# Two result tiles by turns for the expert blocks of a mixture-of-experts stage

## The chip, the core and the metric

The kernel runs on one core of one Trainium2 chip. The metric is the time of one execution on the device in microseconds (us); several runs of the same program are shown by their median. Five engines work side by side, each through its own list of instructions: PE (TensorE, matrix products into PSUM), ACT (ScalarE), DVE (VectorE), POOL (GpSimd, which here issues the gathers and scatters of single rows) and SP (SyncE, which here issues the plain transfers). An instruction that must wait holds up all that stand behind it in its engine's list.

## The reference

One decoder layer on 2048 tokens of width 1024: sliding-window attention beside a chunkwise mLSTM, an output projection, a cross attention to 256 memory slots, a mixture of experts, and a last RMSNorm. What the change touches is the mixture:

```python
hb = jax.nn.silu(xb @ w_g[e]) * (xb @ w_u[e])     # xb: the rows of the tokens of expert e
y = (hb @ w_d[e]) * gate                          # 1024 -> 512 -> 1024
out = zeros((t, d)).at[token].add(y)              # every token goes to two of 32 experts
out = rms_norm(x + out, norm_final)
```

All arithmetic is in float32. The kernel splits every float32 operand into a high and a low part and makes three products of them.

## The kernel before

The expert stage (`phase3`) runs over the 32 experts in a fixed order; x is the place in that order, 0 to 31. Each place x has these blocks of tokens:

- the full block: the first 128 tokens of the expert. `full_gate` and `full_up` make gate and up, `full_down` (with `down_turn`) makes the result in two PSUM tiles of 512 columns, ACT copies both into the tile `yA` in SBUF (line 1755), and POOL adds its rows into the table `y_d` in HBM with an indirect transfer (`add_rows`, line 1788);
- the half block: 64 more tokens, if the expert has more than 128. It stands in the If path of a branch (`half_within`, line 1693); its result goes into `hu`, the upper 64 partitions of the tile `both`. An expert with at most 128 tokens takes the Else path;
- the rare blocks: 64 tokens each, if the expert has more than 192 (`later_blocks`, a branch inside the If path, line 1719; a loop for more than 256 behind a further branch, line 1726). Their result goes into `yA[:64]`. These blocks need the first eight of the twelve weights again, whose split parts have been overwritten: they are read once more through two tiles by turns, `again` and `yA` (`reload`, line 1521), first four of this expert's, then four of the next expert's.

With this seed fifteen places up to 30 take the If path, sixteen the Else path, and one place (x = 2) runs a rare block.

Weights come from HBM in pieces of 512 KB (twelve an expert) into nine buffers `we_raw`; SP issues a piece when its buffer is free. ACT casts a piece to its high part (line 76), DVE makes the low part (line 77). On either path of the branch SP issues four pieces (`splitter(todo[:4])`), the fourth of them a piece of `w_e_up`. Behind the branch stand, in the order written for PE, ACT and DVE: the down products, four casts, the two copies of line 1755, the first products of the next expert (`full_gate`) with four casts and the silu, then its up products, which write the PSUM tiles that the copies read.

POOL's list holds, for each place: the gather of rows for the last norm where a group of experts is done (`sums`, line 1933, which reads `y_d` and so waits for the scatter before it; 15 places between 10 and 29), the gather of the next rows (line 1585), the small steps of the norm, its part of the branch, and the scatter of line 1788.

The waits are put in by the compiler. A transfer tells of its end by raising a counter once its data is in; there are eight such counters for SP's transfers and eight for POOL's, used by turns. What stands behind a branch waits for what either path may have done to its tile. So that a constant can be waited for, the path that did not issue a transfer raises that transfer's counter by hand, at its end (instructions of the lines 1460 and 1719) or ahead of a transfer of its own on the same counter.

Of the kernel before, what the change touches and what calls it, by code (L numbers as in the profile page):

```python
# [31 lines left out]
HB = 64  # L32
# [11 lines left out]
def together(*parts):  # L44

    parts = [iter(p) for p in parts]
    while parts:
        parts = [p for p in parts if next(p, p) is not p]


def by(n, part):

    for i, _ in enumerate(part):
        if i % n == n - 1:
            yield
# [11 lines left out]
class Net:  # L67
# [1675 lines left out]
    def down_turn(self, pd, hT, x, ws, step, norm, late):  # L1743
        for k in range(4):
            self.down(pd, hT, ws, (k,))
            step(2 if k == 1 else 1)
            self.steps(norm, k == 2, late[k])
        info = self.infos[x][0]
        y = self.sums_of.get("A", self.yA)
        for n in range(2):  # L1750
            yn = y[:, n * 512:n * 512 + 512]
            if self.sums_of:
                self.nc.vector.tensor_tensor(out=yn, in0=pd[n], in1=yn, op=ALU.add)
            else:
                self.nc.scalar.copy(out=yn, in_=pd[n])  # L1755
        if self.sums_of:
            out = [(info, self.yA), *self.due]
            self.due = []
            ssq, r = self.stats(P, len(out))
            self.square(y, ssq, 0)  # L1760
            self.gain(self.nc.vector, y, self.yA)
            root = self.root_steps(ssq, r)
            next(root)
            next(root)
            for at, y in out[1:]:
                self.gain(self.nc.vector, y)
            together(by(2, root), norm)
            for j, (at, y) in enumerate(out):
                rj = r[:y.shape[0], j:j + 1]
                if j:  # L1770
                    self.nc.scalar.activation(out=y, in_=y, func=AF.Copy, scale=rj)
                else:
                    self.nc.vector.tensor_scalar(out=y, in0=y, scalar1=rj, scalar2=None, op0=ALU.mult)
                self.give_apart(at, y)
        else:
            self.add_rows(info, y)
# [67 lines left out]
    def half_block(self, tg, info, ws):  # L1844

        h, u, hT = self.half_tiles()
        y = self.yA[:HB, :]
        if self.sums_of:
            self.sums(info, self.sums_of["L"])
        pg = self.pd()  # L1850
        self.gate(pg, tg, ws)
        self.half_silu(h, pg)
        self.half_up(h, u, tg, ws, info)
        pd = [self.pd() for _ in range(2)]
        for f in range(2):
            self.turn_h(h, hT, f)
            self.down(pd, hT, ws, (2 * f, 2 * f + 1))
        self.half_out(y, pd, info, "L")
# [183 lines left out]
```

## Time and profile before

| | |
|---|---|
| median of 3 runs | 2264.99 us (2260.93 to 2270.77) |
| the profiled execution | 2258.9 us, its span 2257.2 us |
| mean granted TensorE clock | 0.963 |
| expert stage | from about 1290 us to the end of the span |
| busy share of the span | PE 91%, DVE 69%, ACT 56%, POOL 21% |

The span goes from the first to the last instruction that the profile holds; the 1.7 us around it belong to the execution's time. Times in the rows count from the span's start.

### The profile page before, as it was taken

The numbers are of one execution on the slowest core, as the hardware profiler recorded it, in microseconds if no ns is written. First come the engines' busy times: TensorE is split into PE (matmuls) and PEld (weight loads), VectorE is DVE, ScalarE is ACT, GpSimd is POOL, SyncE is SP. The second block draws the span as 40 slices with busy tenths as digits, with TensorE's granted clock in tenths as the row PEclk, the third lists the DMA queues.
The fourth block names the chain that finished last, engine by engine and source line by source line (L and its number), as shares of the span: only waits on it lengthen the run. The fifth ranks groups of instructions, "written<-read, shape, count | busy, mean of one in ns | idle before, by whom it ended". The sixth has DMA issues, their size and how long they took to land. (4 is left out here: it accounts for less than half of the span.)

```text
span 2257.2 us, 36582 instructions
## 1 busy us (share of the span) xinstructions
PE 2055.1 (91%) x12173; PEld 1776.2 (79%) x12173; DVE 1555.3 (69%) x3586; ACT 1271.4 (56%) x2479; POOL 466.6 (21%) x536
## 2 busy tenths in 40 slices
PE   6999999999989999999997397799999999899894
PEld 5888888998867887889997285588877887778783
DVE  6277877278866666567777565486777778777764
ACT  6266886268874333355554154476666666666663
POOL 1000000000000000023332211021232426543335
PEclk9999999999999999999999699799999999999997
DMA  5533435443377897523545576496878979897853
GB/s 166 136 112 104 127 101 164 128 112 108 101 196 219 231 227 186 182 103 92 135 77 166 106 258 210 133 351 228 287 266 294 355 235 329 317 355 239 288 185 95
DMA packets 266261, 434.73 MB, mean 193 GB/s; under 512 B 53232, under 2 KB 175216, under 8 KB 265952
## 3 DMA queue, kind: packets, MB, share of 16 engines
q1 hardware_dynamic: 245216, 381.25, 54.8%
q0 software_dynamic: 20736, 49.85, 8.1%
q8 instruction: 134, 2.20, 0.4%
q14 instruction: 175, 1.43, 0.2%
HBM read 356.97 MB, written 92.71 MB: 199 GB/s over the span
## 5 line engine op out<-in xcount | busy, mean ns | idle before, releaser
L77 DVE TENSOR_TENSOR we_lo<-we_raw,we_hi 128x1024 fp32r<-128x1024 f32 x384 | 447.9, 1219 | 95.5 <-ACT we_hi L76 83.7
L76 ACT CAST we_hi<-we_raw 128x1024 fp32r<-128x1024 f32 x384 | 381.9, 1058 | 69.9 <-PE pd L1620 29.8
L125 PE MATMUL pu<-we_hi,xTA 128*128 128x256 f32 x512 | 149.7, 292 | 32.9 <-ACT yA L1755 32.9
L125 PE MATMUL mm<-hT,w_hi 128*128 128x512 f32 x416 | 166.4, 401 | 0.9 <-ACT hT L327 0.9
L126 PE MATMUL mm<-hT,w_hi 128*128 128x512 f32 x416 | 166.0, 399 | 0.0
L127 PE MATMUL mm<-hT,w_lo 128*128 128x512 f32 x416 | 165.9, 399 | 0.0
L127 PE MATMUL mm<-w_hi,hT 128*128 128x324 f32 (+1 forms) x512 | 152.6, 298 | 0.0
L125 PE MATMUL mm<-w_hi,hT 128*128 128x324 f32 (+1 forms) x512 | 152.5, 298 | 0.0
L126 PE MATMUL mm<-w_lo,hT 128*128 128x324 f32 (+1 forms) x512 | 152.1, 297 | 0.0
L126 PE MATMUL pu<-we_lo,xTA 128*128 128x256 f32 x512 | 148.6, 290 | 0.0
L127 PE MATMUL pu<-we_hi,xTA 128*128 128x256 f32 x512 | 148.6, 290 | 0.0
L589 POOL TENSOR_TENSOR sq<-sq 128x256 f32<-128x256 f32 x16 | 12.6, 787 | 588.4 <-ACT sq L586 588.4
L125 PEld LDWEIGHTS pu<-we_hi,xTA 128*128 128x128 f32 x512 | 101.6, 199 | 37.0 <-ACT yA L1755 35.9
L125 PE MATMUL pu<-we_hi,hT 128*128 128x512 f32 x256 | 106.0, 414 | 5.4 <-ACT both L1798 2.2
L126 PE MATMUL pu<-we_lo,hT 128*128 128x512 f32 x256 | 105.1, 410 | 5.2 <-PEq L1719 5.2
L127 PE MATMUL pu<-we_hi,hT 128*128 128x512 f32 x256 | 103.2, 403 | 0.0
L126 PEld LDWEIGHTS pu<-we_lo,xTA 128*128 128x128 f32 x512 | 101.5, 198 | 1.1
L125 PE MATMUL pg<-we_hi,xTA 128*128 128x512 f32 x256 | 101.8, 397 | 0.0
L126 PE MATMUL pg<-we_lo,xTA 128*128 128x512 f32 x256 | 101.4, 396 | 0.0
L127 PE MATMUL pg<-we_hi,xTA 128*128 128x512 f32 x256 | 101.3, 396 | 0.0
L127 PEld LDWEIGHTS pu<-we_hi,xTA 128*128 128x128 f32 x512 | 101.3, 198 | 0.0
L1788 POOL DMA_INDIRECT y_d<-yA,infoA x31 | 71.9, 2320 | 126.0 <-ACT yA L1755 64.6
(508 smaller groups left out, 6081.3 us busy)
## 6 DMA issues: line engine op xcount, KB each, us to landing
we_raw<-in_w_e_gate_dram SPq DMA_DIRECT2D x128, 512.0 KB
we_raw<-in_w_e_up_dram SPq DMA_DIRECT2D x128, 512.0 KB
we_raw<-in_w_e_down_dram SPq DMA_DIRECT2D x128, 512.0 KB
w_raw<-in_w_in_dram SPq DMA_DIRECT2D x56, 256.0 KB
q_in<-q_d SPq DMA_DIRECT2D x32, 256.0 KB
qk_d<-acc SPq DMA_DIRECT2D x32, 256.0 KB
at_d<-at SPq DMA_DIRECT2D x32, 256.0 KB
at_in<-at_d SPq DMA_DIRECT2D x32, 256.0 KB
```

Source lines behind the costliest of these rows:

```text
L76: first = nc.scalar.copy(out=hi, in_=src)
L77: (low or nc.vector).tensor_tensor(out=lo, in0=src, in1=hi.bitcast(F32), op=ALU.subtract)
L125: first = mm(ps, lhsT=wh, rhs=xh, start=start, stop=False)
L126: mm(ps, lhsT=wh, rhs=xl, start=False, stop=False)
L127: mm(ps, lhsT=wl, rhs=xh, start=False, stop=stop)
L589: nc.gpsimd.tensor_tensor(out=sq[:, 0:2], in0=sq[:, 0:2], in1=sq[:, 2:4], op=ALU.add)
L1788: self.nc.gpsimd.indirect_dma_start(out=self.y_d[:, :], out_offset=bass.IndirectOffsetOnAxis(ap=info[:, 0:1], axis=0), in_=y, in_offset=No ...
```

## The change

The full block's result goes into `yA` at even places and into `again` at odd ones. The rare blocks' result goes into `hu`, which holds the same block's gate and up before. Nothing else is edited; at the last place (31) the results go another way (`sums_of`), before as after.

```diff
     def down_turn(self, pd, hT, x, ws, step, norm, late):
...
         info = self.infos[x][0]
-        y = self.sums_of.get("A", self.yA)
+        y = self.sums_of.get("A", (self.yA, self.again)[x % 2])
...
     def half_block(self, tg, info, ws):
 
         h, u, hT = self.half_tiles()
-        y = self.yA[:HB, :]
+        y = self.hu
```

`reload` is not edited, and goes on using both tiles:

```python
        t = (self.again, self.yA)[i % 2]
        self.load_part(x, i, t)
        self.split(*w, t)
```

## Rows read from the trace of the kernel before

**Rows 1.** Stretches: from:to, length, busy us by engine, clock, DMA share, GB/s.

```profile
1455.00:1515.00 60.00, 60.00 (x347) 52.63 (x347) 51.84 (x57) 45.23 (x61) 13.57 (x10) 0.98 1.00 344
...
1875.00:1918.00 43.00, 42.16 (x233) 37.08 (x234) 36.22 (x44) 32.70 (x46) 24.58 (x21) 0.93 0.97 337
```

**Rows 2.** Line 1755: what ended ACT's idle time before it; who waited for it.

```profile
  DMA y_d<-yA,infoA: 15.4, 3
  DMA out_dram<-y_fin,list: 14.3, 2
  SPq L1719: 12.6, 12
...
  PE pu L125: 32.9, 7
```

**Rows 3.** Timeline of PE: start, us, line, operation [idle before, releaser].

```profile
1452.26 0.58 PE L125 MATMUL pu<-we_hi,xTA 128*128 128x256 f32 x1 [11.84 <-ACT yA L1755]
...
1659.30 0.45 PE L1782 MATMUL pt<-ident,hA 128*128 128x128 f32 x1 [3.16 <-DVE hA L1644]
...
1874.72 0.58 PE L125 MATMUL pu<-we_hi,xTA 128*128 128x256 f32 x1 [4.21 <-ACT yA L1755]
...
1969.16 0.58 PE L125 MATMUL pu<-we_hi,xTA 128*128 128x256 f32 x1 [5.29 <-ACT yA L1755]
...
2015.09 0.38 PE L125 MATMUL pu<-we_hi,xTA 128*128 128x256 f32 x1 [1.69 <-ACT yA L1755]
```

**Rows 4.** Timeline of POOL: the rare block's scatter, a full one, the gather behind.

```profile
1433.17 1.43 POOL L1788 DMA_INDIRECT y_d<-yA,infoB  x1 [25.43 <-DVEq L1726]
...
1760.80 1.84 POOL L1788 DMA_INDIRECT y_d<-yA,infoA  x1 [3.95 <-ACT yA L1755]
1771.34 1.02 POOL L1933 DMA_INDIRECT y_fin<-y_d,list  x1 [8.70 <-DMA y_d<-yA,infoA]
```

**Rows 5.** Instructions of line 1460 (Else path's end), 1776 to 1790 us: duration, starts.

```profile
L1460 POOLq INC_SWDGE_SEM  x1: 683/683/683, 1784.2 to 1784.2; - x1
```

**Rows 6.** Timeline of ACT: casts and copies of line 1755 at five places.

```profile
1511.32 0.58 ACT L1755 COPY yA<-pu 128x512 f32<-128x512 f32 x1
...
1761.62 1.05 ACT L76 CAST we_hi<-we_raw 128x1024 fp32r<-128x1024 f32 x1 [0.15 <-DMA we_raw<-in_w_e_gate_dram]
...
1784.99 0.59 ACT L1755 COPY yA<-pu 128x512 f32<-128x512 f32 x1 [4.56 <-DMA y_d<-yA,infoA]
...
1815.68 0.59 ACT L1755 COPY yA<-pu 128x512 f32<-128x512 f32 x1 [0.62 <-SPq L1719]
...
1988.40 0.59 ACT L1755 COPY yA<-pu 128x512 f32<-128x512 f32 x1
```

**Rows 7.** Timeline of SP: issues of reloads and of weight pieces.

```profile
1416.08 0.33 SPq L1516 DMA_DIRECT2D again<-in_w_e_up_dram  x1
...
1437.01 0.33 SPq L1516 DMA_DIRECT2D yA<-in_w_e_up_dram  x1
...
1443.10 0.33 SPq L1516 DMA_DIRECT2D yA<-in_w_e_up_dram  x1
...
1508.87 0.33 SPq L1516 DMA_DIRECT2D we_raw<-in_w_e_up_dram  x1
...
1753.78 0.33 SPq L1516 DMA_DIRECT2D we_raw<-in_w_e_gate_dram  x1
...
1811.22 0.33 SPq L1516 DMA_DIRECT2D we_raw<-in_w_e_up_dram  x1
...
1985.90 0.33 SPq L1516 DMA_DIRECT2D we_raw<-in_w_e_up_dram  x1
```

**Rows 8.** Stretches of 8 us behind two of the waits (columns as above).

```profile
1874.00:1882.00 8.00, 7.28 (x38) 7.28 (x39) 5.12 (x5) 6.68 (x11) 4.02 (x3) 0.57 0.79 249
...
1969.00:1977.00 8.00, 7.84 (x52) 7.84 (x52) 5.28 (x6) 6.22 (x11) 3.47 (x2) 0.75 0.81 253
```

**Rows 9.** The page's costliest group: busy us, mean ns of one, idle before.

```profile
L77 DVE TENSOR_TENSOR we_lo<-we_raw,we_hi 128x1024 fp32r<-128x1024 f32 x384 | 447.9, 1219 | 95.5 <-ACT we_hi L76 83.7
```

## The prediction

> **What bounds the kernel now.** I read the stretches of the expert stage first. Where several places in a row take the Else path, PE is busy nearly all the time (60.0 of 60 us) and the transfers run at 337 to 344 GB/s with 0.97 to 1.00 of the DMA engines' time [rows 1]. Two limits lie on top of each other there: what frees PE meets the transfers at once. That they do bind shows at 1761.62: the cast waited for its own piece, issued at 1753.78, so 7.8 us earlier [rows 6, 7].
>
> Then I read the copies of line 1755, since they alone write the tile that is doubled. PE waited for them seven times, 32.9 us together [rows 2], out of some 960 us of stage. One of the seven, 11.84 us, is at the rare block; two (4.21 and 5.29 us) are at even places, 18 and 22; 1.69 us at place 24 [rows 3]. The rest, 32.9 - 11.84 - 4.21 - 5.29 - 1.69 = 9.9 us, falls on three odd places: 15, 21 and 27.
>
> The reader should see what these copies did not wait for: the scatter of the place before. It went out at 1760.80, and the gather that needs it started at 1771.34, so it was done some 10.5 us later [rows 4]; the copy of place 15 came at 1784.99 after 4.56 us of waiting [rows 6]. By then the scatter had been done for 13 us, although the row puts the wait down to it. What ended just before is POOL's raising of counters by hand at the end of the Else path, 683 ns from 1784.2 [rows 5]: the rare block's scatter, not run here, could have read `yA`, and POOL came late to say that it had not, because its list had stood behind the scatter until 1771.34. So five copies waited for a late POOL, 15.4 + 14.3 = 29.7 us of ACT's time [rows 2].
>
> **The change, part by part.** *No instruction is added or taken away.* Copies, scatters and transfers keep number and size; only waits move.
>
> *The rare block's result in `hu`.* No copy of line 1755 has to hear from POOL's branch any more: the five waits lose their cause. It also frees the reloads. `again` was loaded at 1416.08, `yA` only at 1437.01, since the rare block's scatter (1433.17) was reading `yA`, and the fourth reload went out at 1443.10 [rows 4, 7]. Now the `yA` load follows the first at about 1417, in the cover of the rare block's own products. The two casts follow the block's last copies at about 1433, 1.05 us each, and DVE's part takes 1.2 [rows 6, 9]; so the second tile is free, and the fourth reload goes out, at 1433.2 + 2 x 1.05 + 1.2 = 1436.5 in place of 1443.10. I take 6.5 us. It cannot be more than the 11.84 that PE waits; zero is the other bound, if the casts come later for another cause. `hu` is not late for anyone: the block's gate and up have been transposed before its result is made, and the next half block is four places on.
>
> *Two tiles by turns.* As a cover for the scatter this is worth nothing, as shown. But it changes whose counter the copy waits for, because both tiles are also written by the reloads on the path that is not run. In the order of that path there are thirteen transfers on eight counters by turns: four weight pieces, four reloads, `again`, `yA`, a list of rows (before or after that `yA`), `again`, `yA`. The last `yA` is the thirteenth and shares its counter with the fifth, a reload: on the Else path that counter is raised by hand, early. The last `again` is the twelfth and shares its counter with the fourth: a weight piece that the Else path itself issues. So the copy at an odd place on the Else path will wait until that piece has landed. I take this as forecast.
>
> The Trainium skill states the ground of this wait (DMA: Bandwidth & Descriptors, "Why a DMA increments its semaphore by 16 and not by 1"): only the full count means that the data has landed. No row here shows it for a copy on the Else path; by it the wait lasts to the landing.
>
> *Its price.* On the If path nothing changes: there SP raises all counters in one go behind the same fourth piece, for either tile. Piece at 1811.22, copy at 1815.68, 4.5 us later [rows 6, 7]; twelve copies waited so, 12.6 us in all, with hardly any wait of PE [rows 2]. On the Else path a piece takes longer, 7.8 us by the pair above. That was the first of the four; a piece of 0.524 MB takes 1.5 us at 344 GB/s, while DVE frees a buffer every 1.2 [rows 1, 9], so the fourth falls 3 x 0.3 us further behind: 8.7. Place 5: 1508.87 + 8.7 = 1517.6 against the copy at 1511.32, 6 us late. Place 23: 1985.90 + 8.7 = 1994.6 against 1988.40, 6 us late [rows 6, 7]. Places 3, 9 and 19 have the same form. Of a late copy some is hidden: the five late copies cost ACT 29.7 us and PE 4.21 + 5.29 + 9.9 = 19.4, so 2 us each. Then PE loses 4 us, and after such waits it ran at the half level (1.2 GHz) for a time: mean 0.57 and 0.75 over 8 us, so up to 8 x 0.43 = 3.4 and 8 x 0.25 = 2.0 us lost [rows 8]; for the shorter wait I take the middle between none and 3.4. Together 5.7 us a stall. Bounds for a piece: 4.5 us (the If row: then the copies of these five places are hidden) and 10.2 us, if one gather or scatter of the same size falls among the four.
>
> *What each stall adds.* Places 3 and 5 lie in one stretch with the transfers at their limit [rows 1]; what PE loses at 3 the transfers gain, so that 5 is less late: one stall's 5.7 us for both. Place 9 costs 5.7, but the 3.16 us at 1659.30 [rows 3], where PE stands behind DVE and its pieces a place later, goes: 2.5. At places 15, 21 and 27 the copy already came about when the fourth piece lands: POOL's wait goes, the piece's takes its seat, 0. Places 18 and 22 are even and are freed: 4.21 + 5.29 and 3.4 + 2.0 us of low clock, 14.9. But 19 and 23 follow, whose copies cannot come before their piece, and the pieces come no earlier in a stretch with 0.97 of the DMA time used [rows 1]. So the gain is taken back at the next place; what stands at place 24 is the stall of 23, 5.7, less the 1.69 that 24 then doesn't wait [rows 3]: +4.0.
>
> Sum: -6.5 + 5.7 + 2.5 + 0 + 4.0 = +5.7 us. On the profiled execution, 2258.9 + 5.7 = 2264.6; that execution lies 6.1 under the median and 2.0 under the fastest of the runs shown, and the median with the sum is 2270.7. I say 2268, between the two.
>
> **The rivals.**
>
> *The double tile does what double tiles do: faster.* The copy at odd places doesn't wait for the fourth piece, because the compiler counts the reload's counter otherwise. For it: on the old tile the copy waits for a counter raised by hand. Against: order and number of the transfers. Then the rare block's 6.5, the 9.9 of the odd places and the 14.9 of the even ones are there to win, 31 us; with 0.97 of the DMA time used [rows 1] much of what PE is freed of runs into pieces, and I take two thirds, 21: 2238 on the profiled execution, 2244 on the median. The Trainium skill (Trainium Kernel Development and Optimization, Best Practices) states the rule behind this rival: double-buffer, to overlap transfers with compute. By it alone the time would fall; the rows of the scatter speak against it here.
>
> *The stalls add up: slower.* If the pieces are issued later when PE and ACT stand, they don't gain what PE loses. Then all five stalls cost 5.7 each: 28.5 - 6.5 = +22, 2281 to 2287. Decided at place 5: whether its copy comes at 1517.6, counted from place 3 as now, or 4 us after. For it: a piece goes out only when DVE has freed a buffer, and DVE follows ACT.
>
> *Nothing moves.* POOL's lateness also holds a list load on SP, and pieces behind it; freed copies run into pieces that are late for the same cause, and the fourth piece lands early enough. -6.5 to 0: 2258 to 2265.
>
> **How the numbers follow.** The forecast 0.62 (2256 to 2280), faster rival 0.15, slower rival 0.15, nothing moves 0.08. A bound of 0.5% is 11.3 us; less than that a measurement here can't tell from no change. Faster: 0.14 of the first rival and 0.01 of the rest, 0.15. Slower: 0.14 of the second and about 0.08 of the forecast, where a piece takes 10.2 us and the rare block gives nothing, 0.22. Same: 0.63. The range, 2242 to 2284, has the upper edge of the first rival and half of the slower one in it.
>
> **What would show it.** Right: the rare block's second reload straight behind its first, PE's 11.84 us halved; no copy of line 1755 waiting for POOL; at places 3, 5, 9, 19 and 23 new waits of 3 to 8 us for a `w_e_up` piece, and half-level clock behind them; even places without wait. Wrong: odd Else places without wait, or places 18 to 24 ending earlier by more than 5 us on their own count.

## The result and the profile after

The changed kernel takes 2280.16 us (median of 6 runs, 2272.14 to 2284.54); the kernel before, run beside it, 2262.04 (6 runs, 2258.55 to 2270.77). The ratio is 1.0068, 95% interval 1.0050 to 1.0086: slower by 15 us by this ratio (the recorded ratio is not the quotient of the two medians, which lie 18.1 us apart), a little over the half per cent that the prediction counts as a change, with the interval's lower end on that bound. The forecast was 2268, so sign and mechanism hold and the size does not: +5.7 us forecast, +15 measured. 2280.16 lies at the upper edge of what the forecast gave itself (2256 to 2280), and "slower" had been given 0.22. One run of a kernel below (places 15, 21 and 27 in `again`) took 3185.32 us at a granted clock of 0.585; it is left out of that kernel's median and ratio as a slow one. Between the two profiled executions the span grew from 2257.2 to 2278.3, so by 21.1 us; 2.2 of it lie ahead of the first copy of line 1755, where nothing was changed.

The waits of that line's copies in the changed kernel, beside [rows 2]: what ended ACT's idle time before them, and who waited for them (us, times).

```profile
L1755 ACT COPY yA<-pu x32: 582/592/618, 1339.4 to 2221.6; 128x512 f32<-128x512 f32 x32
L1755 ACT COPY again<-pu x30: 586/590/594, 1371.2 to 2190.2; 128x512 f32<-128x512 f32 x30
its engine sat idle before it (us, times) until:
  DMA we_raw<-in_w_e_up_dram: 50.1, 8
  SPq L1719: 13.4, 13
who waited for it (us, times):
...
  PE pu L125: 45.5, 9
```

POOL is gone from the list: the five waits of 29.7 us are no more. In their place stand eight waits, 50.1 us, for a `w_e_up` piece. The timeline of ACT shows where: copies at places 5, 15, 18, 23 and 27.

```profile
1516.92 1.07 ACT L1755 COPY again<-pu 128x512 f32<-128x512 f32 x2 [7.43 <-DMA we_raw<-in_w_e_up_dram]
...
1793.95 1.07 ACT L1755 COPY again<-pu 128x512 f32<-128x512 f32 x2 [5.82 <-DMA we_raw<-in_w_e_up_dram]
...
1878.54 1.10 ACT L1755 COPY yA<-pu 128x512 f32<-128x512 f32 x2
...
2011.08 0.59 ACT L1755 COPY again<-pu 128x512 f32<-128x512 f32 x1 [7.23 <-DMA we_raw<-in_w_e_up_dram]
...
2125.08 1.07 ACT L1755 COPY again<-pu 128x512 f32<-128x512 f32 x2 [7.29 <-DMA we_raw<-in_w_e_up_dram]
```

All eight odd places on the Else path (3, 5, 9, 15, 19, 21, 23, 27) wait so, 3.3 to 8.3 us; the eight even ones do not wait at all. PE's timeline, at the rare block and behind the copies of places 3, 5, 15, 19, 21 and 23, beside [rows 3]:

```profile
1448.74 0.58 PE L125 MATMUL pu<-we_hi,xTA 128*128 128x256 f32 x1 [6.21 <-ACT yA L1755]
...
1471.58 0.39 PE L125 MATMUL pu<-we_hi,xTA 128*128 128x256 f32 x1 [1.31 <-ACT again L1755]
...
1517.56 0.58 PE L125 MATMUL pu<-we_hi,xTA 128*128 128x256 f32 x1 [5.29 <-ACT again L1755]
...
1794.59 0.58 PE L125 MATMUL pu<-we_hi,xTA 128*128 128x256 f32 x1 [4.63 <-ACT again L1755]
...
1908.94 0.58 PE L125 MATMUL pu<-we_hi,xTA 128*128 128x256 f32 x1 [4.53 <-ACT again L1755]
...
1957.04 0.58 PE L125 MATMUL pu<-we_hi,xTA 128*128 128x256 f32 x1 [6.39 <-ACT again L1755]
...
2011.72 0.58 PE L125 MATMUL pu<-we_hi,xTA 128*128 128x256 f32 x1 [8.63 <-ACT again L1755]
```

At the rare block 11.84 us became 6.21. SP's issues there say why, beside [rows 7], and give the piece for which place 5 waits:

```profile
1418.41 0.33 SPq L1516 DMA_DIRECT2D again<-in_w_e_up_dram  x1
1419.55 0.33 SPq L1516 DMA_DIRECT2D yA<-in_w_e_up_dram  x1
1436.67 0.33 SPq L1516 DMA_DIRECT2D again<-in_w_e_up_dram  x1
1437.80 0.33 SPq L1516 DMA_DIRECT2D yA<-in_w_e_up_dram  x1
...
1509.60 0.33 SPq L1516 DMA_DIRECT2D we_raw<-in_w_e_up_dram  x1
```

The `yA` load goes out 1.1 us behind the one into `again`; before, it was 20.9. The piece issued at 1509.60 landed at 1516.83 by the transfer's record, and the copy started at 1516.92. At each of the six odd places for which the trace holds this record (5, 9, 15, 21, 23, 27) the copy starts 0.10 us after the landing. The rule that the prediction took from the Trainium skill (DMA: Bandwidth & Descriptors, "Why a DMA increments its semaphore by 16 and not by 1"), by which the wait lasts to the landing, agrees.

Stretches of the changed kernel (columns as in [rows 1]); the last line is the kernel before:

```profile
1455.00:1515.00 60.00, 55.23 (x312) 47.01 (x310) 47.42 (x53) 40.00 (x53) 17.27 (x8) 1.00 0.95 328
...
1471.00:1479.00 8.00, 6.68 (x54) 6.51 (x55) 5.51 (x6) 5.56 (x8) 1.60 (x1) 1.00 1.00 316
1517.00:1525.00 8.00, 7.44 (x51) 7.44 (x51) 5.12 (x5) 5.27 (x7) 1.60 (x1) 0.79 0.91 306
...
1870.00:2040.00 170.00, 143.44 (x779) 124.05 (x778) 127.80 (x151) 111.72 (x157) 75.89 (x91) 0.90 0.92 320
...
2011.00:2019.00 8.00, 7.28 (x46) 7.28 (x47) 5.12 (x5) 5.34 (x7) 3.65 (x2) 0.71 0.97 247
...
1870.00:2040.00 170.00, 149.59 (x849) 128.85 (x848) 128.93 (x162) 112.93 (x164) 88.15 (x98) 0.95 0.91 324
```

The first stretch, full before [rows 1], now has 4.8 us without a product. Over the 8 us behind place 3's wait the clock is 1.00, behind place 5's 0.79, behind place 23's 0.71. From 1870 to 2040 its mean is 0.90; the kernel before has 0.95 there.

### The profile page after: what moved, and what is told of

It reads as the page before. It is cut to its first block, busy times and chain, and to the rows that moved or that the text cites. A ratio compares the mean times of both kernels' runs of the same rounds, so it can differ in the third digit from the quotient of the medians.

```text
span 2278.3 us, 36567 instructions
## 1 busy us (share of the span) xinstructions
PE 2062.0 (91%) x12173; PEld 1781.9 (78%) x12173; DVE 1557.7 (68%) x3586; ACT 1270.1 (56%) x2479; POOL 454.8 (20%) x536
## 5 line engine op out<-in xcount | busy, mean ns | idle before, releaser
L125 PE MATMUL pu<-we_hi,xTA 128*128 128x256 f32 x512 | 153.1, 299 | 45.5 <-ACT again L1755 39.3
L127 PE MATMUL pu<-we_hi,xTA 128*128 128x256 f32 x512 | 151.2, 295 | 0.0
L125 PEld LDWEIGHTS pu<-we_hi,xTA 128*128 128x128 f32 x512 | 104.7, 204 | 50.4 <-ACT again L1755 42.7
L127 PEld LDWEIGHTS pu<-we_hi,xTA 128*128 128x128 f32 x512 | 104.3, 204 | 0.0
L76 ACT CAST hT<-pt 128x256 fp32r<-128x256 f32 x64 | 23.9, 373 | 133.5 <-PE pt L1782 133.5
```

The costliest lines, as they stand in the source:

```text
L76: first = nc.scalar.copy(out=hi, in_=src)
L125: first = mm(ps, lhsT=wh, rhs=xh, start=start, stop=False)
L127: mm(ps, lhsT=wl, rhs=xh, start=False, stop=stop)
```

## The experiments

Theory A: the loss is the wait of the copies into `again` for the Else path's fourth piece, and it is there because the last reload of `again` is the twelfth transfer on eight counters. Theory B: the rare result in `hu`, or the reloads that it moves, costs the time. Rival C: the wait belongs to the tile, whichever counter is used. Then there is the question of size: do stalls add up, or share?

Ratios are against the kernel before, run beside each kernel on the same chip, with 95% intervals. Its median is 2263.61 (15 runs) beside the first four kernels, 2266.8 (24) beside the next four and 2266.76 (7) beside the last two.

**Each half alone.** `hu` alone:

```diff
-        y = self.sums_of.get("A", (self.yA, self.again)[x % 2])
+        y = self.sums_of.get("A", self.yA)
```

> Theory A: all that the change costs comes from the turns, since the copy to `again` waits for the Else path's fourth weight piece; the rare result in `hu` only gains. Then with `hu` alone and all full results in `yA`, no copy of line 1755 waits for a w_e_up piece (50.1 us of ACT at 8 places in the changed kernel) nor for POOL (29.7 us in the kernel before); PE's waits for that line fall from 45.5 to under 10 us (6 of it at the rare block), and the time is under that of before: 6 us at the rare block and one to two thirds of the 19.4 us and the low clock behind them, 2238 to 2256. Theory B: the result in `hu`, or the reloads that it moves, carries the loss; then this kernel is as slow as the changed one, 2272 to 2285.

Measured: 2249.63 us, ratio 0.9930 (0.9905 to 0.9955). The waits of line 1755 in it:

```profile
L1755 ACT COPY yA<-pu x62: 574/591/619, 1344.9 to 2193.8; 128x512 f32<-128x512 f32 x62
its engine sat idle before it (us, times) until:
  SPq L1719: 13.8, 12
  SPq L1460: 2.8, 3
who waited for it (us, times):
...
  PE pu L125: 9.2, 5
```

Theory B falls; this version beats both kernels. And the turns alone:

```diff
-        y = self.hu
+        y = self.yA[:HB, :]
```

> The turns without `hu`. Theory A: at the eight odd Else places the same waits for the w_e_up piece (some 50 us of ACT, 39 of PE); at the even places 18, 22 and 24 the waits for POOL's hand-raised counters are back (4.2, 5.3 and 1.7 us of PE before), and at the rare block 11.8 us in place of 6.2: PE's waits for line 1755 some 55 to 62 us, the time 2283 to 2298. Theory B (`hu` is to blame): 2255 to 2268.

Measured: 2279.84, ratio 1.0073 (1.0045 to 1.0100); the waits for the piece are 47.3 us at 8 places, and PE waits 52.2 us for the line. The rare block's 11.85 us and POOL's waits at places 18 and 22 are back, as expected, but the time is that of the changed kernel; it and PE's 52.2 us are both under what I expected. From place 17 to 26 it takes 237.9 us and the changed kernel 240.2: the odd copies come when their piece lands, and in these two executions the waits ahead of them make no difference.

**The counter or the tile.** The reloads in the other order:

```diff
-        t = (self.again, self.yA)[i % 2]
+        t = (self.yA, self.again)[i % 2]
```

> The changed kernel with the reloads in the other order, `yA` first, so that the last load into `yA` is the twelfth transfer and that into `again` the thirteenth. Theory A (the counter of the twelfth transfer is shared with the fourth weight piece): the waits for the w_e_up piece move from the eight odd Else places to the eight even ones, 4, 10, 12, 14, 18, 20, 22 and 24, and none is left at an odd place; some 40 to 55 us of ACT, the time 2265 to 2290. Rival C (the wait belongs to the tile `again`, not to a counter's place in the turn): waits stay at the odd places, 2272 to 2285.

Measured: 2287.36, ratio 1.0091 (1.0058 to 1.0125). ACT at places 4 and 5, and the sum over the line:

```profile
1497.32 0.58 ACT L1755 COPY yA<-pu 128x512 f32<-128x512 f32 x1 [6.79 <-DMA we_raw<-in_w_e_up_dram]
...
1517.61 0.59 ACT L1755 COPY again<-pu 128x512 f32<-128x512 f32 x1
...
  DMA we_raw<-in_w_e_up_dram: 58.8, 8
```

The wait has moved from `again` to `yA`, from odd to even places: exactly the eight named, and none else. Then one 32-byte transfer more, ahead of the reloads, which runs once in this kernel (its lines are shifted by two from there, 1755 is 1757):

```diff
             self.again = t("again", [P, D])
+            self.spare = t("spare", [P, 8])
...
         with self.tc.If(cnt > P + HB, label=f"most{x}"):
+            self.nc.sync.dma_start(out=self.spare[0:1, :], in_=self.a["w_e_down"][0, ORDER[x], 0:1, 0:8])
             for i, _ in enumerate(over):
```

> The changed kernel with one more transfer, of 32 bytes, ahead of the reloads on the rare block's path, which with this seed is issued once; the last loads into `again` and `yA` become the thirteenth and fourteenth and share their counters with the fifth and sixth, reloads that the Else path does not issue. Theory A: no copy of line 1755 waits for a w_e_up piece, at odd or even places; PE's waits for that line under 10 us; 2238 to 2256, as with `hu` alone. If the second tile is worth something of its own, it is below the run with `hu` alone by over 5 us. Rival C: the waits at the odd places stay, and 2272 to 2285.

Measured: 2249.36, ratio 0.9930 (0.9905 to 0.9955). The issue of the small transfer, and the waits of the copies:

```profile
1401.09 0.31 SPq L1721 DMA_DIRECT2D spare<-in_w_e_down_dram  x1
...
L1757 ACT COPY again<-pu x30: 585/592/626, 1373.4 to 2164.2; 128x512 f32<-128x512 f32 x30
its engine sat idle before it (us, times) until:
  SPq L1720: 8.8, 8
  SPq L1461: 5.7, 5
```

All eight waits for a piece are gone, and 31 us with them (PE still waits 11.5 us for the line, where I expected under 10). Rival C falls. And with two tiles by turns, now free of that wait, the time is the same as with one tile (2249.36 and 2249.63): the second tile is worth nothing that shows here.

**What each stall costs.** Four kernels with `hu`, all results in `yA` but for the places named, which go to `again`; for the first:

```diff
-        y = self.sums_of.get("A", (self.yA, self.again)[x % 2])
+        y = self.sums_of.get("A", self.again if x in (3, 5) else self.yA)
```

> The kernel with `hu` alone (2249.6), but with the full results of places 3 and 5 in `again`, so that only these two copies wait for the fourth piece. Sharing (the prediction's step): what PE loses at 3 the transfers gain, so that 5 is less late; one stall for both, +5.7: 2255. Adding up: both stand as in the changed kernel, PE 1.3 and 5.3 us, and the low clock behind the longer one, up to 3.4 us: +8 to 11, 2258 to 2261. In the profile: from the copy of place 2 to that of place 6, 91.9 us with `hu` alone, is 97 to 98 by sharing and 100 to 103 by adding up.

> The same with place 9 alone in `again`. Prediction's step: a stall of 5.7 us less what the next place gives back (3.2), +2.5: 2252. Adding up: +5.7 with nothing given back, 2255. From the copy of place 8 to that of place 11, 76.9 us with `hu` alone: 79 or 83.

> The same with places 15, 21 and 27 in `again`. Prediction's step: here the copy of the kernel before already came about when the fourth piece lands, so this costs only what POOL's waits cost there, some 6 to 8 us of the 14 that `hu` alone gained on the kernel before: 2256 to 2258. Against it: the piece lands later than POOL's wait ended, as the 4.6, 6.4 and 5.5 us of PE in the changed kernel say: +12 to 20 with the low clock, 2262 to 2270.

> The same with places 19 and 23 in `again`. Prediction's step: their pieces come no earlier than now, so that these copies give back only the time by which the places before had gained: about the time of the kernel before at place 24 plus 4.0, so +5 to 10 on `hu` alone: 2255 to 2260. Adding up: the 4.5 and 8.6 us of PE in the changed kernel and the low clock behind them: +13 to 20, 2263 to 2270. If the four groups (3 and 5; 9; 15, 21 and 27; 19 and 23) add up to about 30 us, the stalls are independent of each other; if to much less, they feed one another; if to much more, they share.

Measured: 2255.78, 2250.19, 2262.81 and 2260.24 us; ratios 0.9944 (0.9923 to 0.9964), 0.9923 (0.9906 to 0.9941), 0.9968 (0.9951 to 0.9984), 0.9969 (0.9953 to 0.9985). Against the 0.9930 of `hu` alone that is +3, -2, +9 and +9 us, each uncertain by some 7. Together they make 19, where the changed kernel has 31; but the error of `hu` alone is in this sum four times, so that it is uncertain by some 24 and does not tell adding up from sharing. By the ranges put down before, +9 fits the prediction's step for places 19 and 23 (+5 to 10), and lies between the step (6 to 8) and its rival (12 to 20) for 15, 21 and 27; with 7 us of uncertainty these are hints.

So I take lengths of stretches, from the start of one place's first copy of line 1755 to another's, worked out from the starts in the timelines. They are of one execution each, and such an execution can lie well off its kernel's median (that of places 15, 21 and 27 is 8 us faster):

| us from place to place | 0 to 2 | 2 to 6 | 8 to 11 | 14 to 17 | 17 to 26 | 26 to 28 | 0 to 30 |
|---|---|---|---|---|---|---|---|
| before | 114.4 | 91.2 | 77.2 | 88.4 | 231.5 | 57.6 | 863.1 |
| changed kernel | 108.7 | 99.6 | 77.6 | 93.2 | 240.2 | 59.5 | 881.7 |
| `hu` alone | 106.3 | 91.9 | 76.9 | 88.0 | 226.8 | 57.1 | 848.4 |
| turns alone | 114.1 | 100.8 | 78.6 | 92.8 | 237.9 | 59.3 | 884.0 |
| one more transfer | 110.0 | 91.1 | 79.0 | 88.1 | 225.8 | 59.3 | 854.4 |
| places 3, 5 | 108.3 | 99.5 | 73.6 | 87.3 | 224.4 | 57.7 | 851.9 |
| place 9 | 105.9 | 91.3 | 78.7 | 90.1 | 225.9 | 56.2 | 848.3 |
| places 15, 21, 27 | 108.7 | 92.8 | 72.9 | 91.7 | 231.7 | 57.0 | 855.3 |
| places 19, 23 | 107.2 | 93.0 | 76.3 | 87.4 | 238.1 | 57.0 | 860.1 |
| other reload order | 109.8 | 97.9 | 83.9 | 85.7 | 238.9 | 56.8 | 888.9 |
| all in `again` | 107.1 | 100.0 | 82.4 | 87.9 | 241.4 | 55.8 | 891.8 |
| all in `again`, one more transfer | 109.0 | 92.5 | 74.2 | 84.4 | 228.4 | 57.9 | 852.4 |

Where nothing stalls, a stretch still differs from kernel to kernel: by 2 us from 2 to 6, by 3 from 26 to 28, by 4 from 17 to 26, by 6 from 8 to 11 and from 14 to 17. Places 3 and 5 cost 7.6 us (99.5 less 91.9): between the 97 to 98 us that I expected from sharing and the 100 to 103 from adding up. Place 9 takes 1.8, which is near the prediction's +2.5 but within the spread of its stretch. 15 costs 3.7, at the edge of the spread (the changed kernel's 93.2 and the 92.8 with the turns alone lie beyond it), 21 costs 4.9 (231.7 less 226.8), 27 nothing that shows, 19 and 23 together 11.3. The groups make 29.3 together; the changed kernel has 29.4 over `hu` alone in the same stretches. So between these groups no sharing shows.

**All places at once.** Every full result in `again`, and the same with the small transfer:

```diff
-        y = self.sums_of.get("A", (self.yA, self.again)[x % 2])
+        y = self.sums_of.get("A", self.again)
```

> All full results in `again`, none in `yA`: every one of the sixteen Else places waits for its fourth piece. Adding up: the eight odd places cost 33 us of stage against `hu` alone (881.7 less 848.4 us from the copy of place 0 to that of place 30), the eight even ones, from the run with the other reload order, 40.6 us (889.0 less 848.4); both together some 74, so 2315 to 2330. Sharing: in a stretch of Else places one after another (3 to 5, 18 to 24) a place that waits finds its next pieces nearer, so that the second and third wait less; then 2285 to 2305, and the ACT waits for the w_e_up piece are well under 50.1 + 58.8 us.

> The same with the extra 32-byte transfer ahead of the reloads. If only the shared counter makes the copies wait, all sixteen waits are gone and the time is that of `hu` alone, 2242 to 2257, although one single tile takes all results and is a tile of the reloads. If the tile matters, it stays near the run without the extra transfer.

Measured: 2292.15, ratio 1.0118 (1.0099 to 1.0138), and 2253.25, ratio 0.9939 (0.9922 to 0.9955). In the first, ACT's copies at places 3, 4 and 5, and the sum over the line:

```profile
1469.37 0.58 ACT L1755 COPY again<-pu 128x512 f32<-128x512 f32 x1 [4.22 <-DMA we_raw<-in_w_e_up_dram]
...
1492.78 0.58 ACT L1755 COPY again<-pu 128x512 f32<-128x512 f32 x1 [4.08 <-DMA we_raw<-in_w_e_up_dram]
...
1515.34 0.58 ACT L1755 COPY again<-pu 128x512 f32<-128x512 f32 x1 [3.17 <-DMA we_raw<-in_w_e_up_dram]
...
  DMA we_raw<-in_w_e_up_dram: 87.9, 16
```

Sixteen waits cost 43 us over `hu` alone (891.8 less 848.4), not 74; the wait at 4 is 4.08 us here and 6.79 where 4 waits without 3 and 5. So stalls at places next to each other share. From 2 to 6, place 4 alone costs 6.0 us, 3 and 5 cost 7.6, all three 8.1. From 17 to 26, place 21 costs 4.9, 19 and 23 cost 11.3, 19, 21 and 23 cost 13.4, all seven 14.6. The one tile with the small transfer is as fast as `hu` alone within the intervals: neither the number of tiles nor the tile shows in the time, only the counter's place in the turn.

## Why the prediction was right in kind and short in size

- **No copy waits for the scatter; five wait for POOL's late counters.** Right: with `hu` alone these waits are gone. Their price was small: from place 2 to 30 the kernel before takes 748.6 us and `hu` alone 742.1, so 29.7 us of ACT's waiting were worth 6.5 (4.2 by the kernel with one more transfer, 744.4). What took the rest back is shown below.
- **The rare block: -6.5.** Right: PE's wait went from 11.84 to 6.21 us, the stretch from 0 to 2 from 114.4 to 108.7.
- **The odd Else copy waits for the fourth piece, by the shared counter.** Right, and shown by moving it and by taking it away. It was there at all eight odd places. From issue to landing the six records give 7.2, 7.4, 10.4, 8.1, 10.7 and 9.6 us (places 5, 9, 15, 21, 23, 27), mean 8.9: the estimate was 8.7, good as a mean, but they range over 3.5 us.
- **Places 3 and 5 share: +5.7.** Measured +8.4 (99.6 less 91.2). That 5 is less late because 3 stalled is not shown. PE stood 1.31 us behind 3, with the clock at 1.00 for the next 8 us, and 5.29 behind 5, with 0.79: 1.3 + 5.3 + 8 x 0.21 = 8.3, with nothing shared. The two cost less than two stalls of 5.7 because the one at 3 is short; no run has either place alone. The sign named for place 5 is met from the copy of place 3 (46.0 us, 45.9 forecast); from that of place 2 it is 68.8, between the 66.0 of sharing and the 70.0 of adding up. Place 9: +2.5 forecast, +0.4 measured, +1.8 with place 9 alone, both within the spread of that stretch.
- **Places 15, 21 and 27: 0. This step failed at 15 and 21.** It took the copy of the kernel before as coming about when the piece lands. By the records of that kernel the piece landed after the copy: at 15 at 1786.85, 1.85 us after the copy [rows 6], at 21 1.2 us. In the changed kernel it came later still: from the copy of 14 to that of 15 it is 29.0 us, before 25.6, and then 32.8 to the copy of 16, before 30.7. From 14 to 17: +4.8. At 27 the step holds: the piece had landed 0.5 us ahead of the copy, and from the copy of 26 it is 26.8 us, before 26.6.
- **Places 18 to 24: +4.0.** That nothing stands of the 14.9 us freed at 18 and 22 is right. That 19 and 23 take it back is only part of it: with `hu` alone, where neither waits for its piece, 17 to 26 takes 226.8 us after 231.5, so there were not 14.9 us to win but 4.7. The size is wrong: from 17 to 26 it is +8.6, place 21 in it. At 23 the piece took 10.7 us, not 8.7; in the kernel before, by its records, it took 10.1 already (issued at 1985.90, last recorded part at 1996.03). PE stood 8.63 us in place of 4, and the mean clock of the stretch fell from 0.95 to 0.90, 8.5 us of full speed over 170 us; with `hu` alone it is 0.97:

```profile
1870.00:2040.00 170.00, 151.94 (x862) 128.91 (x861) 133.55 (x166) 115.20 (x163) 70.83 (x99) 0.97 0.93 329
```

- **The sum.** By stretches the change gave -5.7, +8.4, +0.4, +4.8, +8.6, +1.9 (26 to 28) and +0.2 in the rest: +18.6 in this execution, where -6.5 + 5.7 + 2.5 + 0 + 4.0 = +5.7 was forecast. The two terms that were short by most are 15 with 21 and 27 (0) and 18 to 24 (+4.0), together by 11 (1.9 of it at 26 to 28, within the spread of that stretch).
- **The rivals.** "The stalls add up" gave the better number, 2281. Its reason holds in part: between the odd places no sharing shows, but places next to each other do share, and it too left out 15 and 21. "Nothing moves" (2258 to 2265) falls. "The double tile does what double tiles do" falls twice: the odd copies did wait, and without that wait two tiles gave what one gives, since at place 15 of the kernel before the scatter had been done for 13 us when the copy came. The rule cited beside this rival (the Trainium skill, Trainium Kernel Development and Optimization, Best Practices: double-buffer) finds nothing here to overlap.

**Why waits for POOL cost so little.** The record shows what took their place. From the copy of place 2 to that of place 30, what PE waited for (us, times, longest), and the stretch with its columns as in [rows 1]: first the kernel before, then the changed one, then `hu` alone.

```profile
PE pu L125 <- ACT yA L1755: 32.9, 7, 11.8
PE pt L1782 <- DVE hA L1644: 8.1, 7, 3.2
...
1451.62:2200.27 748.65, 706.48 (x4049) 600.58 (x4050) 563.66 (x714) 490.64 (x716) 267.01 (x303) 0.98 0.84 288
...
PE pu L125 <- ACT again L1755: 39.3, 8, 8.6
PE pt L1782 <- DVE hA L1644: 7.8, 5, 3.2
...
1448.10:2221.11 773.01, 712.77 (x4045) 606.61 (x4046) 564.44 (x715) 489.83 (x716) 254.02 (x303) 0.96 0.82 279
...
PE pt L1782 <- DVE hA L1644: 24.0, 13, 4.2
PE pu L125 <- ACT yA L1755: 9.2, 5, 6.1
...
1451.25:2193.34 742.09, 702.40 (x4045) 594.88 (x4046) 565.03 (x715) 492.28 (x717) 253.99 (x303) 0.98 0.85 290
```

Without the rare block's wait (11.8 and 6.1) PE waited 21.1 us for the copies in the kernel before and 3.1 with `hu` alone. Of these 18.0 us, 15.9 come back as waits for `hA`, the product of gate and up that DVE makes: 24.0 after 8.1. So PE's idle time falls by 2.5 us only (42.2 to 39.7). The waits for a piece take `hA`'s place as well (7.8), but are longer: against `hu` alone the changed kernel idles 20.5 us more, and its PE is busy 10.4 us longer for the same number of products, at a mean clock of 0.96 after 0.98. By this one execution of each, some third of the 30.9 us goes with the lower clock.

Open: what makes `hA` late when the copies are on time, and whether the stall of 3 makes that of 5 shorter. No run here tells.

## What to carry to other kernels

Before a tile gets a second use, list all that ever writes or reads it, the paths that seldom run too: on the path that is taken, its next user waits for the counter of that other transfer, and where counters go by turns this can be the counter of an unrelated transfer that has just been issued. Look for what the wait really ends on before a second buffer is given to it; here to untie the rare path (`hu` alone) was worth 0.7%, and the second buffer nothing. Where a copy is to come "about when" a transfer lands, read the landing from the trace, since two microseconds at a place decide. And what a wait is worth that you take away shows only in what its engine waits for next.

## What the runs showed that was not expected

Nothing in the prediction led to this, though the run that shows it was expected to come out so: one transfer of 32 bytes, 0.31 us on SP and run once, made the kernel 31 us faster (2280.16 to 2249.36), for it moved the rest of that path by one place in the turn of counters. Stalls in a run of Else places level off: one, two and three waits between places 2 and 6 cost 6.0, 7.6 and 8.1 us, where that stretch differs by 2 without them. And of 18.0 us of waits for copies that fell away with `hu` alone, PE spent 15.9 waiting for `hA`.
